# Norms by two float32r products and a full-width inverse root, and operands a multiple of 64 bytes apart

## The chip, the cores and the metric

The kernel runs on one core of a Trainium2 chip (trn2). TensorE (PE) multiplies, VectorE (DVE), ScalarE (ACT) and GpSimd (POOL) work on tiles of 128 partitions, and SyncE (SP) issues most DMAs. The metric is the device time of one execution in microseconds; lower is better.

## The reference

One decoder layer over a sequence of 1024 tokens with 1024 features, in float32. Six of its steps are RMS norms over the features of x:

```python
def rms_norm(x, g):
    xf = x.astype(jnp.float32)
    y = xf * lax.rsqrt(jnp.mean(xf * xf, axis=-1, keepdims=True) + NORM_EPS)
    return (y * g.astype(jnp.float32)).astype(x.dtype)

def swiglu(u, w_in, w_out):
    gate, up = jnp.split(u @ w_in, 2, axis=-1)
    return (jax.nn.silu(gate) * up) @ w_out

# reference(), one layer
f1 = swiglu(rms_norm(h, ffn1_pre_g[l]), ffn1_w_in[l], ffn1_w_out[l])
h = h + HALF_STEP * rms_norm(f1, ffn1_post_g[l])
u = rms_norm(h, mix_pre_g[l])
p_rwkv, p_swa, q_mem, gate_logits = _split(u @ w_in[l], IN_SIZES)
...
mem_n = rms_norm(mem, mem_norm_g[l])
...
h = h + rms_norm(merged @ w_out[l], mix_post_g[l])
f2 = swiglu(rms_norm(h, ffn2_pre_g[l]), ffn2_w_in[l], ffn2_w_out[l])
h = h + HALF_STEP * rms_norm(f2, ffn2_post_g[l])
```

The mixer between them has three branches: a recurrence over 64-feature heads (RWKV-7), windowed attention and attention into 256 memory tokens `mem`. NORM_EPS is 1e-6; the feed-forward width is 2816.

## The kernel before

Activations lie feature-major: a tile holds 128 features (partitions) of 512 tokens (columns), and x is eight such tiles for each half h of the sequence. A weight product is done in three float32r products (`mm3`, L327 to L332): the weight and the moving operand are each split into a rounded part (`hi`) and its remainder (`lo`), the copy to `hi` on ScalarE, the subtraction to `lo` on VectorE (`split` L392, `operand` L261), and hi·hi, hi·lo and lo·hi are summed in PSUM. Weights come through five staging buffers (`w_raw`) and up to eight split operands (`w_hi`, `w_lo`), each for twelve products.

The stages follow each other: the norm of `mem` with its keys and values, the first FFN (nine column blocks of its gate products first, `ffn_in_gate`, then the rest; its output in seven forms, `ffn_outs`, summed by `ffn_out_sum`), the mixer, the output projection (`pw`), the second FFN, whose last output form runs for two quarters of 256 columns (TAIL), so that the last norm covers only 256 columns.

A norm over x has these steps. `sum_squares` (L396) squares the eight tiles on ScalarE and adds them on VectorE. `rstd` (L358) then sums over the 128 partitions by products: for each 128 columns the squares are the stationary operand and a column of ones the moving one (`ps_ms`, L365), so that the sums come out as a column on 128 partitions, four columns for 512 tokens. Thirteen small VectorE instructions on 128 x 4 elements make the inverse root (a start from the bit pattern, three Newton steps); in the last stage (`quick`) a reciprocal, ScalarE's Sqrt and one step. Four products with the identity (`ps_rs`, L387) then spread the roots over all partitions, into PSUM. `pre_norm` (L410), `factors_norm` (L441) and `post_norm` (L719) multiply each tile by its gain and by this bank; `post_norm` adds the residual and stores. There are thirteen such norms: eleven over 512 columns, two over 256 in the tail; `mem` has one of its own (`start`).

The operands of `ps_ms` and `ps_rs` are float32. The tile framework orders the instructions of each engine by a priority: inside `high_priority` they are put ahead by `self.lead` or `self.urgent`, and `keep_in_program_order` keeps those it is given in the written order. `between` is work that PE is given between the two blocks of a norm, at the start and in the tail. PSUM has eight banks: four with the tag `mm` (`px`, `py`, `pr`, `pq`, `pw`, `po` and others), four for the rest.

Tiles of a pool lie one behind the other in SBUF, so a pool's addresses depend on the sizes before it. `ones` and `gn_eps` are tiles of one float32 column.

Of the kernel before, what the change touches and what calls it, by code (L numbers as in the profile page):

```python
# [10 lines left out]
F32 = mybir.dt.float32  # L11
F32R = mybir.dt.float32r
I32 = mybir.dt.int32
ALU = mybir.AluOpType
ACT = mybir.ActivationFunctionType
AXX = mybir.AxisListType.X

P = 128
T = 1024
TH = 512  # L20
D = 1024
# [3 lines left out]
MEM = 256  # L25
EPS = 1e-6
# [72 lines left out]
class WindowBlock(Block):  # L99
# [10 lines left out]
    def scores(self):  # L110
        nc, V, S, k = self.nc, self.nc.vector, self.nc.scalar, self.k
        self.w0 = P if self.b == 0 else 0
# [3 lines left out]
        for kv in (0, 1):  # L116
            for q in (0, 1):
                ps = k.psum("sc")
                rows = slice(q * 64, q * 64 + 64)
                for j in (0, 1):  # L120
                    last = self.mm(ps[:, j * n : (j + 1) * n], self.qs[rows, kv * 2 + j], self.kd[kv][rows, kcols])
                i = (kv * 2 + q) * 2
                V.scalar_tensor_tensor(sc[:, i : i + 2, :n], ps[:, : 2 * n].rearrange("p (j k) -> p j k", k=n), 0.125,
                                       k.wmask[:, self.w0:].rearrange("p k -> p () k").broadcast_to([P, 2, n]), ALU.mult, ALU.add)
        st = self.pool.tile([P, 5, 8], F32, tag="st", name="st", bufs=2)
        V.tensor_reduce(st[:, 0], sc[:, :, :n], AXX, ALU.max)
        V.tensor_tensor(st[:, 0], st[:, 0], k.sinks, ALU.max)
        V.tensor_scalar(st[:, 1], st[:, 0], -1.0, None, ALU.mult)
        V.tensor_tensor(st[:, 2], k.sinks, st[:, 0], ALU.subtract)
        S.activation(st[:, 2], st[:, 2], ACT.Exp)  # L130
# [77 lines left out]
class Builder:  # L208
# [146 lines left out]

    def rstd(self, sqs, width, pool, n=TH, columns=False, quick=False, between=None):  # L358
        nc = self.nc
        V = nc.vector  # L360
        nb = n // P
        ps = self.psum("ps_ms")
        for j in range(nb):
            for i, sq in enumerate(sqs):
                mm = nc.tensor.matmul(ps[:, j : j + 1], sq[:, j * P : (j + 1) * P], self.ones, start=i == 0, stop=i == len(sqs) - 1)  # L365
                if between:
                    self.tc.keep_in_program_order(mm)
        m, y, hm, q = (pool.tile([P, 4], F32, tag="rs" + t, name="rs" + t, bufs=2)[:, :nb] for t in "myhq")
        with self.tc.high_priority(offset=self.lead):
            V.tensor_scalar(m, ps[:, :nb], 1.0 / width, EPS, ALU.mult, ALU.add)  # L370
            if quick:
                V.reciprocal(y, m)
                nc.scalar.activation(y, y, ACT.Sqrt)
            else:
                V.tensor_scalar(y.bitcast(I32), m.bitcast(I32), 1, None, ALU.logical_shift_right)
                V.tensor_scalar(y.bitcast(I32), y.bitcast(I32), -1, 0x5F3759DF, ALU.mult, ALU.add)
            V.tensor_scalar(hm, m, -0.5, None, ALU.mult)
            for _ in range(1 if quick else 3):
                V.tensor_tensor(q, y, y, ALU.mult)
                V.tensor_tensor(q, q, hm, ALU.mult)  # L380
                V.scalar_tensor_tensor(y, q, 1.5, y, ALU.add, ALU.mult)
        if between:
            between()
        out = self.psum("ps_rs")
        with self.tc.high_priority(offset=self.lead):
            for j in range(nb):
                mm = nc.tensor.matmul(out[:, j * P : (j + 1) * P], y[:, j : j + 1].broadcast_to([P, P]), self.ident, start=True, stop=True)  # L387
                if between:
                    self.tc.keep_in_program_order(mm)
        return (out, y) if columns else out  # L390

    def split(self, x, hi, lo):  # L392
        self.nc.scalar.copy(hi, x)  # L393
# [2 lines left out]
    def sum_squares(self, xs, pool):  # L396

        nc = self.nc
        n = xs[0].shape[1]
        acc = None  # L400
        for x in xs:
            sq = pool.tile([P, n], F32, tag=f"sq{n}", name="sq", bufs=3)
            nc.scalar.activation(sq, x, ACT.Square)
            if acc is None:
                acc = sq
            else:
                nc.vector.tensor_tensor(acc, acc, sq, ALU.add)
        return acc

    def pre_norm(self, x, part, gname, u, pool):  # L410

        h, lo, hi = part
        xs = [t[h][:, lo:hi] for t in x]
        rs = self.rstd([self.sum_squares(xs, pool)], D, pool, hi - lo)[:, : hi - lo]
        for k in range(KD):
            if lo == 0:
                u[k][h] = self.u_tile(), self.u_tile()
            t = pool.tile([P, TH], F32, tag="un", name="un", bufs=2)[:, : hi - lo]
            self.nc.vector.scalar_tensor_tensor(t, xs[k], self.vec(gname, k), rs, ALU.mult, ALU.mult)
            self.split(t, *(y[:, lo:hi] for y in u[k][h]))  # L420
# [20 lines left out]
    def factors_norm(self, xs, part, gname, pool, between=None, then=None):  # L441

        h, lo, hi = part
        xs = [x[h][:, lo:hi] for x in xs]
        rs = self.rstd([self.sum_squares(xs, pool)], D, pool, hi - lo, between=between)[:, : hi - lo]
        for k in range(KD) if then else (0, 4, 1, 5, 2, 6, 3, 7):
            self.nc.vector.scalar_tensor_tensor(xs[k], xs[k], self.vec(gname, k), rs, ALU.mult, ALU.mult)
            if then:
                then(k)
# [269 lines left out]
    def post_norm(self, acc, part, gcol, xr, pool, save=None):  # L719

        nc = self.nc
        h, lo, hi = part
        cols = slice(h * TH + lo, h * TH + hi)
        xs = [acc[k][h][:, lo:hi] for k in range(KD)]
        end = save is self.io["out"]
        with self.tc.high_priority(offset=self.urgent if end else 0):
            sq = self.sum_squares(xs[KH:] + xs[:KH] if h else xs, pool)
        rs = self.rstd([sq], D, pool, hi - lo, quick=end, between=self.between if end else None)[:, : hi - lo]
        for k in range(KD):
            nc.vector.scalar_tensor_tensor(xs[k], xs[k], gcol(k), rs, ALU.mult, ALU.mult)  # L730

            e = nc.gpsimd if end and cols.stop == T and k in (0, 2, 4) else nc.vector
            e.tensor_tensor(xs[k], xs[k], xr[k], ALU.add)
            if save is not None:
                nc.sync.dma_start(save[:, k, cols], xs[k])
# [5 lines left out]
    def mixer_consts(self, cp):  # L741
        nc, io = self.nc, self.io
        V = nc.vector
# [15 lines left out]
        for q in (0, 64):  # L759
            for i, op in ((0, ALU.is_gt), (1, ALU.is_ge)):  # L760
                m = self.gmask[q : q + 64, i, :]
# [23 lines left out]
        m = self.wmask[:, :P]  # L785
        nc.gpsimd.affine_select(m, m, [[1, P]], ALU.is_gt, NEG, base=0, channel_multiplier=-1)
        m = self.wmask[:, P:]
        nc.gpsimd.affine_select(m, m, [[-1, P]], ALU.is_ge, NEG, base=0, channel_multiplier=1)
        self.gn_eps = cp.tile([P, 1], F32, name="gn_eps")
        V.memset(self.gn_eps, GN_EPS)  # L790


# [394 lines left out]
    def start(self, x, pool, km_d, vm_d):  # L1187
        nc, tc, io = self.nc, self.tc, self.io
        V = nc.vector
        keep = tc.keep_in_program_order  # L1190
        send = self.send = lambda *a: keep(nc.sync.dma_start(*a))
        mm = lambda *a, start, stop: keep(nc.tensor.matmul(*a, start=start, stop=stop))
# [7 lines left out]
        def load_x(h, a):  # L1200
            for k in range(a, a + KH):
                send(x[k][h], io["xT"][:, k, h * TH : (h + 1) * TH])
# [32 lines left out]
        def mem_squares():  # L1235
            out = []
            for a in (0, KH):
                sq = pool.tile([P, KH, MEM], F32, tag="mem_sq", name="mem_sq", bufs=1)
                s = pool.tile([P, MEM], F32, tag="mem_ss", name="mem_ss", bufs=2)
                nc.scalar.activation(sq, mem[:, a : a + KH], ACT.Square)  # L1240
                V.tensor_tensor(sq[:, :2], sq[:, :2], sq[:, 2:], ALU.add)
                V.tensor_tensor(s, sq[:, 0], sq[:, 1], ALU.add)
                out.append(s)
            return out
# [12 lines left out]
        sqs = mem_squares()  # L1257
# [5 lines left out]
        keys(2)  # L1263
        load_strip()
        load_x(1, 0)
        ps, col = self.rstd(sqs, D, pool, MEM, True, between=while_mem)
        load_x(1, KH)
        rs = pool.tile([P, MEM], F32, name="mem_rs", bufs=1)
        nc.scalar.copy(rs, ps[:, :MEM])
        for h in range(4):  # L1270
            t = pool.tile([P, MEM], F32, tag="km", name="km", bufs=2)
# [5 lines left out]
        for i in (0, 1):  # L1277
            t = pool.tile([P, 512], F32, tag="mkv", name="vm", bufs=3)
# [249 lines left out]
    def build(self):  # L1528
        nc, tc, io = self.nc, self.tc, self.io
        with contextlib.ExitStack() as outer, tc.tile_pool(reuse_waits="tile", name="consts", bufs=1) as cp, \  # L1530
# [5 lines left out]
            nc.scalar.dma_start(self.vecs, io["vecs"])  # L1536
            self.ones = cp.tile([P, 1], F32, name="ones")
            nc.vector.memset(self.ones, 1.0)
            self.ident = cp.tile([P, P], F32, name="ident")
            nc.gpsimd.memset(self.ident, 1.0)  # L1540
            nc.gpsimd.affine_select(self.ident, self.ident, [[1, P]], ALU.is_equal, 0.0, base=0, channel_multiplier=-1)
# [16 lines left out]
            with quarters() as self.qpool:  # L1558
                x = self.acc_tiles()
# [17 lines left out]
            with quarters() as self.qpool:  # L1577
                merged = self.last_branches(*mixed)
                x = self.acc_tiles()
# [90 lines left out]
```

## Time and profile before

| | |
|---|---|
| median of three runs | 2317.04 us (2313.6 to 2322.88) |
| the profiled execution | 2322.86 us, its span 2321.1 us |
| granted TensorE clock | 0.997 |
| busy share of the span | PE 98%, DVE 71%, ACT 41%, POOL 4% |
| HBM | 179 GB/s over the span |

Durations below come from the one profiled execution; the span runs from its first to its last instruction. A product's busy time has a modelled end, so distances between starts are used where PE's time is counted. A matmul of float32 operands appears as two passes in the trace, one of float32r as one.

### The profile page before, as it was taken

Reading aid. Unit: us, or ns where it says so; the run is one execution under the profiler, and the core shown is the slowest. Engines: PE = TensorE matmul, PEld = TensorE weight load, DVE = VectorE, ACT = ScalarE, POOL = GpSimd, SP = SyncE. Lnnn points to the kernel's source line nnn. Section 1 sums busy time; section 2 is a strip of 40 time slices with the busy share of each in tenths; the row PEclk is TensorE's granted clock in tenths of the full one; section 3 lists DMA queues with packets and bytes.
Section 4 is the critical chain, followed back from the end, with each engine's and each line's share of the span. In section 5 each row is a group of like instructions: output and inputs, shape, how many; then the busy total and the mean of one; then the engine's idle time right before and its main releaser. Section 6 shows DMA issues by size and latency. Waiting matters only on the chain. (4 is left out here: it accounts for less than half of the span.)

```text
span 2321.1 us, 33883 instructions
## 1 busy us (share of the span) xinstructions
PE 2278.9 (98%) x12080; PEld 1862.7 (80%) x12080; DVE 1653.6 (71%) x2790; ACT 962.3 (41%) x1791; POOL 95.7 (4%) x134
## 2 busy tenths in 40 slices
PE   8999999999999999999999999999999999999998
PEld 6778888888888777888878888778888778888887
DVE  6998666666688786895645466565899886666666
ACT  5522333454445544223444455234552223345451
POOL 0000000000000000001310000241000000000000
PEclk9999999999999999999999999999999999999999
DMA  8577545586644446325435425555467775558663
GB/s 276 160 251 255 171 158 166 171 289 207 190 160 144 111 118 186 131 96 183 139 130 179 129 95 170 173 178 160 158 212 229 263 243 172 168 182 271 214 195 114
DMA packets 280778, 417.70 MB, mean 180 GB/s; under 512 B 82304, under 2 KB 104320, under 8 KB 280352
## 3 DMA queue, kind: packets, MB, share of 16 engines
q1 hardware_dynamic: 231552, 388.20, 51.9%
q10 hardware_dynamic: 49056, 27.34, 4.2%
q8 instruction: 95, 1.56, 0.3%
q14 instruction: 75, 0.61, 0.1%
HBM read 284.89 MB, written 129.50 MB: 179 GB/s over the span
## 5 line engine op out<-in xcount | busy, mean ns | idle before, releaser
L264 ACT CAST w_hi<-w_raw 128x512 fp32r<-128x512 f32 x594 | 366.2, 620 | 774.8 <-PE px L331 140.9
L266 DVE TENSOR_TENSOR w_lo<-w_raw,w_hi 128x512 fp32r<-128x512 f32 x594 | 415.4, 702 | 218.0 <-ACT w_hi L264 181.1
L330 PE MATMUL po<-u,w_hi 128*128 128x512 f32 (+1 forms) x476 | 181.8, 382 | 0.0
L332 PE MATMUL po<-u,w_lo 128*128 128x512 f32 (+1 forms) x476 | 181.1, 380 | 0.0
L331 PE MATMUL po<-u,w_hi 128*128 128x512 f32 (+1 forms) x476 | 181.0, 380 | 0.0
L330 PE MATMUL pgate<-u,w_hi 128*128 128x512 f32 x384 | 155.2, 404 | 0.0
L332 PE MATMUL pgate<-u,w_lo 128*128 128x512 f32 x384 | 151.5, 394 | 0.0
L331 PE MATMUL pgate<-u,w_hi 128*128 128x512 f32 x384 | 149.7, 390 | 0.0
L330 PE MATMUL px<-f,w_hi 128*128 128x512 f32 x352 | 139.0, 395 | 6.4 <-DVE up L600 3.9
L330 PE MATMUL px<-u,w_hi 128*128 128x512 f32 x352 | 137.5, 391 | 3.0 <-ACT w_hi L264 2.1
L331 PE MATMUL pz<-u,w_hi 128*128 128x512 f32 x352 | 137.3, 390 | 0.6 <-DVE u L394 0.6
L331 PE MATMUL px<-f,w_hi 128*128 128x512 f32 x352 | 137.6, 391 | 0.0
L330 PE MATMUL pz<-u,w_hi 128*128 128x512 f32 x352 | 137.3, 390 | 0.3 <-DVE m L587 0.3
L332 PE MATMUL px<-f,w_lo 128*128 128x512 f32 x352 | 137.5, 391 | 0.0
L331 PE MATMUL px<-u,w_hi 128*128 128x512 f32 x352 | 137.0, 389 | 0.0
L332 PE MATMUL pz<-u,w_lo 128*128 128x512 f32 x352 | 137.0, 389 | 0.0
L332 PE MATMUL px<-u,w_lo 128*128 128x512 f32 x352 | 137.0, 389 | 0.0
L394 DVE TENSOR_TENSOR u<-hid,u 128x512 fp32r<-128x512 f32 x114 | 78.5, 689 | 49.2 <-ACT u L393 46.6
L331 PEld LDWEIGHTS po<-u,w_hi 128*128 128x128 f32 x476 | 89.5, 188 | 17.3
L332 PEld LDWEIGHTS po<-u,w_lo 128*128 128x128 f32 x476 | 89.5, 188 | 17.3
L330 PEld LDWEIGHTS po<-u,w_hi 128*128 128x128 f32 x476 | 89.5, 188 | 17.2
L393 ACT CAST u<-hid 128x512 fp32r<-128x512 f32 x114 | 70.7, 620 | 69.6 <-DMA hid<-form_d 61.8
(347 smaller groups left out, 5127.6 us busy)
## 6 DMA issues: line engine op xcount, KB each, us to landing
w_raw<-in_ffn_in SPq DMA_DIRECT2D x220, 256.0 KB
hid<-form_d SPq DMA_DIRECT2D x154, 256.0 KB
w_raw<-in_win SPq DMA_DIRECT2D x112, 256.0 KB
ws<-in_ffn_out SPq DMA_DIRECT2D x88, 256.0 KB
form_d<-g SPq DMA_DIRECT2D x88, 256.0 KB
ffn_sum_d<-ws SPq DMA_DIRECT2D x88, 256.0 KB
w_raw<-ffn_sum_d SPq DMA_DIRECT2D x88, 256.0 KB
form_d<-h SPq DMA_DIRECT2D x66, 256.0 KB
```

The source lines that it names most:

```text
L264: self.nc.scalar.copy(hi, x)
L266: self.nc.vector.tensor_tensor(lo, x, hi.bitcast(F32), ALU.subtract)
L330: mm(out, wh, xh, start=first, stop=False, **kw)
L331: mm(out, wh, xl, start=False, stop=False, **kw)
L332: mm(out, wl, xh, start=False, stop=last, **kw)
L393: self.nc.scalar.copy(hi, x)
L394: self.nc.vector.tensor_tensor(lo, x, hi.bitcast(F32), ALU.subtract)
```

## The change

The norms over x no longer use `rstd`, which remains for `mem` alone. A new `inverse_root` takes the sum of squares (128 x n), and

- splits it, with the epsilon added, into `sq_hi` (ScalarE) and `sq_lo` (VectorE);
- multiplies both by a constant 128 x 128 float32r matrix `mean_r` of 1/D, so that each row of the PSUM bank `ps_rs` holds the mean over all features: two float32r products of n columns;
- takes the logarithm of that bank and the exponential of -0.5 times it on ScalarE, n columns wide, with one table set loaded ahead (`preload_act_table_set`);
- refines by one Newton step (a square on ScalarE, two VectorE instructions), into the SBUF tile `rs`, from which the users read.

The products stand within `high_priority`; the hi and lo products stand in the written order only where there is a `between`. The squares' ring has four buffers instead of three and now holds `sq_hi`, `sq_lo` and `rs` as well. `gn_eps` and the new `eps` take 16 columns (64 bytes) each, of which one is used.

```diff
-    def rstd(self, sqs, width, pool, n=TH, columns=False, quick=False, between=None):
+    def rstd(self, sqs, width, pool, n, between):
...
+    def inverse_root(self, sq, pool, between=None):
+
+        nc = self.nc
+        n = sq.shape[1]
+        hi, lo, y = (pool.tile([P, n], t, tag=f"sq{n}", name=name, bufs=4) for t, name in ((F32R, "sq_hi"), (F32R, "sq_lo"), (F32, "rs")))
+        ps = self.psum("ps_rs")[:, :n]
+        V, S = nc.vector, nc.scalar
+        keep = self.tc.keep_in_program_order
+        with self.tc.high_priority(offset=self.lead):
+            keep(S.activation(hi, sq, ACT.Identity, bias=self.eps))
+            V.scalar_tensor_tensor(lo, sq, self.eps, hi.bitcast(F32), ALU.add, ALU.subtract)
+            keep(S.preload_act_table_set("natural_log_exp_and_others"))
+            for i, x in enumerate((hi, lo)):
+                mm = nc.tensor.matmul(ps, self.mean_r, x, start=i == 0, stop=i == 1)
                 if between:
-                    self.tc.keep_in_program_order(mm)
-        return (out, y) if columns else out
+                    keep(mm)
+            keep(S.activation(y, ps, ACT.Ln))
+            keep(S.activation(y, y, ACT.Exp, scale=-0.5))
+            keep(S.activation(sq, y, ACT.Square))
+            V.scalar_tensor_tensor(sq, ps, -0.5, sq, ALU.mult, ALU.mult)
+            V.scalar_tensor_tensor(y, sq, 1.5, y, ALU.add, ALU.mult)
+        if between:
+            between()
+        return y
...
-            sq = pool.tile([P, n], F32, tag=f"sq{n}", name="sq", bufs=3)
+            sq = pool.tile([P, n], F32, tag=f"sq{n}", name="sq", bufs=4)
...
-        rs = self.rstd([self.sum_squares(xs, pool)], D, pool, hi - lo)[:, : hi - lo]
+        rs = self.inverse_root(self.sum_squares(xs, pool), pool)
...
-        rs = self.rstd([self.sum_squares(xs, pool)], D, pool, hi - lo, between=between)[:, : hi - lo]
+        rs = self.inverse_root(self.sum_squares(xs, pool), pool, between)
...
-        rs = self.rstd([sq], D, pool, hi - lo, quick=end, between=self.between if end else None)[:, : hi - lo]
+        rs = self.inverse_root(sq, pool, self.between if end else None)
...
-        self.gn_eps = cp.tile([P, 1], F32, name="gn_eps")
+        self.gn_eps = cp.tile([P, 16], F32, name="gn_eps")[:, :1]
...
-        ps, col = self.rstd(sqs, D, pool, MEM, True, between=while_mem)
+        ps, col = self.rstd(sqs, D, pool, MEM, while_mem)
...
+            self.mean_r = cp.tile([P, P], F32R, name="mean_r")
+            nc.vector.memset(self.mean_r.bitcast(F32), 1.0 / D)
+            self.eps = cp.tile([P, 16], F32, name="eps")[:, :1]
+            nc.vector.memset(self.eps, EPS * D / P)
```

More of the change, by code (lines that the diff above doesn't have):

```diff
@@ L364, in rstd @@
             for i, sq in enumerate(sqs):
-                mm = nc.tensor.matmul(ps[:, j : j + 1], sq[:, j * P : (j + 1) * P], self.ones, start=i == 0, stop=i == len(sqs) - 1)
-                if between:
-                    self.tc.keep_in_program_order(mm)
+                keep(nc.tensor.matmul(ps[:, j : j + 1], sq[:, j * P : (j + 1) * P], self.ones, start=i == 0, stop=i == len(sqs) - 1))
         m, y, hm, q = (pool.tile([P, 4], F32, tag="rs" + t, name="rs" + t, bufs=2)[:, :nb] for t in "myhq")
@@ L370, in rstd @@
             V.tensor_scalar(m, ps[:, :nb], 1.0 / width, EPS, ALU.mult, ALU.add)
[L371 to L376, printed above, removed]
+            V.tensor_scalar(y.bitcast(I32), m.bitcast(I32), 1, None, ALU.logical_shift_right)
+            V.tensor_scalar(y.bitcast(I32), y.bitcast(I32), -1, 0x5F3759DF, ALU.mult, ALU.add)
             V.tensor_scalar(hm, m, -0.5, None, ALU.mult)
-            for _ in range(1 if quick else 3):
+            for _ in range(3):
                 V.tensor_tensor(q, y, y, ALU.mult)
@@ L381, in rstd @@
                 V.scalar_tensor_tensor(y, q, 1.5, y, ALU.add, ALU.mult)
-        if between:
-            between()
+        between()
         out = self.psum("ps_rs")
@@ L386, in rstd @@
             for j in range(nb):
-                mm = nc.tensor.matmul(out[:, j * P : (j + 1) * P], y[:, j : j + 1].broadcast_to([P, P]), self.ident, start=True, stop=True)
-                if between:
-                    self.tc.keep_in_program_order(mm)
-        return (out, y) if columns else out
+                keep(nc.tensor.matmul(out[:, j * P : (j + 1) * P], y[:, j : j + 1].broadcast_to([P, P]), self.ident, start=True, stop=True))
+        return out, y
+    def inverse_root(self, sq, pool, between=None):
[4 more added lines that the diff above has]
+        V, S = nc.vector, nc.scalar
+        keep = self.tc.keep_in_program_order
+        with self.tc.high_priority(offset=self.lead):
[4 more added lines that the diff above has]
+                mm = nc.tensor.matmul(ps, self.mean_r, x, start=i == 0, stop=i == 1)
+                if between:
+                    keep(mm)
[5 more added lines that the diff above has]
+        if between:
+            between()
+        return y
     def split(self, x, hi, lo):
```

## The prediction

> **What bounds the kernel now.** I read the page first, then TensorE's waits, then the timeline around single norms.
>
> ```profile
> span 2321.1 us, 33883 instructions
> PE 2278.9 (98%) x12080; PEld 1862.7 (80%) x12080; DVE 1653.6 (71%) x2790; ACT 962.3 (41%) x1791; POOL 95.7 (4%) x134
> PEclk9999999999999999999999999999999999999999
> ...
> PE ps_ms L365 <- DVE sq L407: 3.1, 3, 1.6
> ...
> PE ps_rs L387 <- DVE rsy L381: 2.2, 4, 1.4
> ```
>
> TensorE (PE) is busy for 98% of the span at full granted clock, and stands only some microseconds for the norm: 3.1 for the sum of squares, 2.2 for the root. So the kernel is a queue of products: time goes where a product leaves that queue, or where PE is made to stand. VectorE (DVE, 71%) and ScalarE (ACT, 41%) matter only where they make PE stand, and in the tail after the last product.
>
> The page's busy time has modelled ends, so I count PE time from start to start. Two places in the timeline, one for each kind of norm product:
>
> ```profile
> 1667.40 0.39 PE L331 MATMUL px<-u,w_hi 128*128 128x512 f32 x1
> 1667.63 0.39 PE L332 MATMUL px<-u,w_lo 128*128 128x512 f32 x1
> 1668.13 1.02 PE L365 MATMUL ps_ms<-ones,sq 128*128 128x1 f32 x8
> 1669.01 0.48 PE L330 MATMUL px<-u,w_hi 128*128 128x512 f32 x1
> 1669.33 0.39 PE L331 MATMUL px<-u,w_hi 128*128 128x512 f32 x1
> ...
> 2259.75 0.39 PE L331 MATMUL po<-u,w_hi 128*128 128x512 f32 x1
> 2259.97 0.39 PE L332 MATMUL po<-u,w_lo 128*128 128x512 f32 x1
> 2260.20 1.05 PE L387 MATMUL ps_rs<-ident,rsy 128*128 128x128 f32 x8
> 2261.01 0.48 PE L330 MATMUL po<-u,w_hi 128*128 128x512 f32 x1
> 2261.33 0.39 PE L331 MATMUL po<-u,w_hi 128*128 128x512 f32 x1
> ```
>
> A float32r product of 512 columns starts 0.23 us after the one before it. Around 2260.20 the step from 2259.97 to 2261.33 is 1.36 us and holds two such products (0.46) and one block of norm products: the block costs 0.90 us. In it are eight passes (four float32 products, two passes each), and the first float32r product behind them takes 0.32 instead of 0.23. Around 1668.13 the same sum gives 1.70 - 0.46 = 1.24: 0.90 and a wait of 0.34.
>
> **The change, part by part.**
>
> *Products removed.* `rstd` issues two blocks for each norm over x: `ps_ms` (the mean) and `ps_rs` (the spread of the root over 128 rows). There are thirteen such norms: eleven of 512 columns, two of 256 in the tail. That is 22 blocks at 0.90 = 19.8 us, and four blocks of half the passes. Of these the tail's last two stand behind the last weight product and are counted below; the other two are taken at half, 0.45 each. Together 20.7 us off PE's queue. Mem's norm keeps its blocks.
>
> *Products added.* Each norm gets two float32r products of the same width as its columns, 0.23 us each at 512: 11 x 0.46 = 5.1; the 256 wide pair in the middle of the tail about 0.23. Together 5.3 us. They have the form of the products around them, so the 0.09 us behind a float32 block is gone, and is in the 0.90. Net off PE: 15.4 us.
>
> *Waits at the norm's products.* Before, PE stands for the sum of squares ahead of `ps_ms` and for `rsy` ahead of `ps_rs`; after, for `sq_hi` (ScalarE) and `sq_lo` (VectorE). In the built order most `sq_hi` products are moved forward to where their sum of squares is just ready, and `sq_lo` follows two or three products (0.5 to 0.7 us) behind, about one VectorE instruction of that width. Two meeting points stay two; I set the change at nothing, with 6 us to the good (all of 24 waits of about 0.25) and 6 to the bad.
>
> *The chain to the root.* Rows for its parts, the last two from VectorE's timeline:
>
> ```profile
> L403 ACT ACTIVATE sq<-acc 128x512 f32<-128x512 f32 x88 | 54.3, 630 | 27.4 <-DVE acc L733 9.7 <-DVE acc L685 8.0 <-DVE sq L407 7.8
> ...
> L403 ACT ACTIVATE sq<-acc 128x256 f32<-128x256 f32 x16 | 6.6, 417 | 30.8 <-DVE acc L685 28.6 <-DVE sq L407 1.2 <-DVE rsm L370 0.9
> ...
> L882 ACT ACT_TABLE_LOAD x4 | 5.1, 1283 | 0.1
> ...
> L407 DVE TENSOR_TENSOR sq<-sq 128x512 f32<-128x512 f32 x77 | 53.0, 689 | 9.8 <-ACT sq L403 6.6
> ...
> L730 DVE SCALAR_TENSOR_TENSOR acc<-acc,post,ps_rs 128x512 f32<-128x512 f32 x24 | 17.0, 741 | 1.5 <-PE ps_rs L387 1.5
> ...
> L381 DVE SCALAR_TENSOR_TENSOR rsy<-rsq,rsy 128x4 f32<-128x4 f32 x31 | 5.0, 162 | 1.0
> ...
> 2311.81 0.16 DVE L380 TENSOR_TENSOR rsq<-rsq,rsh 128x2 f32<-128x2 f32 x1
> 2312.01 0.16 DVE L381 SCALAR_TENSOR_TENSOR rsy<-rsq,rsy 128x2 f32<-128x2 f32 x1
> ```
>
> Before: 0.9 of PE, thirteen small VectorE instructions that wait for each other (0.16 each, 0.20 apart: 2.5), 0.9 of PE: 4.3 us. After: `sq_hi` 0.63, `sq_lo` 0.69, product 0.4, logarithm, exponential and square 0.63 each, two instructions of VectorE 0.74 + 0.69: 5.0 us. So the result is some 0.7 us later when nothing else is queued. For VectorE itself 2.5 us of small work become 2.1 of wide work, and eight users read the root from SBUF instead of PSUM (0.74 against 0.69), 0.4 us less: no loss. ScalarE gains 4 x 0.63 and sixteen more table loads (16 become 32 in the built program) of 1.28: 11 x 2.5 + 2 x 1.7 + 20.5 = 51 us in 2321, and it is 41% busy. Its copies `w_hi` run up to eight operands ahead, and an operand lasts twelve products, 2.7 us; a chain of 5 us is covered. Behind the logarithm, which waits for PE's product, stand such copies, and in the gate stage the copies of `px` that free PE's banks. No DMA is added or moved to another queue; ScalarE's own stores of mem's keys and values start later by the chain, and are read in the attention, long after. The chain is not covered where ScalarE is full, nor where PE soon reads what the norm made. The first rows are three stretches with the busy time of each engine, the last two from the timeline:
>
> ```profile
> core 0: us, PE busy (x) PEld busy (x) DVE busy (x) ACT busy (x) POOL busy (x), PEclk, DMA share, GB/s
> 41.00:62.00 21.00, 19.25 (x88) 15.81 (x89) 14.56 (x28) 14.26 (x25) 0.00 (x0) 1.00 0.63 214
> ...
> 690.00:745.00 55.00, 54.39 (x253) 44.52 (x253) 46.74 (x94) 26.72 (x48) 1.12 (x2) 1.00 0.45 144
> 1600.00:1662.00 62.00, 61.43 (x286) 50.56 (x285) 45.93 (x91) 30.50 (x54) 0.00 (x0) 1.00 0.48 153
> ...
> 737.38 0.39 PE L330 MATMUL pr<-u,w_hi 128*128 128x512 f32 x1
> ...
> 738.62 1.29 DVE L394 TENSOR_TENSOR u<-un,u 128x512 fp32r<-128x512 f32 x2
> ```
>
> From 41 to 62 us ScalarE has 14.3 of 21 us. From 690 to 745 VectorE has 46.7 of 55, and the last two tiles of `u` are split at 739.9, while `pr`, begun at 737.38, reads the last of them after 21 products, at 742.2: 2.3 us of slack. Between the norm before it and this place PE loses two to four of its own blocks, 1.3 us each net, which were part of the cover; where that is more than the slack and the chain isn't shorter, PE stands. I take 1.5 us in all; bounds 0 and 6 (the four norms there at 1.5).
>
> *The tail.* Behind the last weight product there is no cover:
>
> ```profile
> 2309.80 0.43 DVE L407 TENSOR_TENSOR sq<-sq 128x256 f32<-128x256 f32 x1 [0.54 <-ACT sq L403]
> 2310.38 0.58 PE L365 MATMUL ps_ms<-ones,sq 128*128 128x1 f32 x4 [1.58 <-DVE sq L407]
> ...
> 2313.04 1.26 DVE L730 SCALAR_TENSOR_TENSOR acc<-acc,post,ps_rs 128x256 f32<-128x256 f32 x3 [0.87 <-PE ps_rs L387]
> ```
>
> From the end of the sum (2310.23) to its first user is 2.81 us. After: `sq_hi` 0.42, then the table load 1.28 (longer than `sq_lo` and the products beside it), three ScalarE steps of 0.42, two of VectorE at about 0.43, and handoffs of about 0.1 in all: 3.9 to 4.1. Plus 1.2 us.
>
> Does a load cost more than its row? Two rows of a switch:
>
> ```profile
> 52.25 1.28 ACT L566 ACT_TABLE_LOAD   x1
> 53.55 0.63 ACT L566 ACTIVATE g<-g 128x512 f32<-128x512 f32 x1
> ```
>
> The next instruction starts 1.30 us after the load does. The Trainium skill, "ScalarE: Activation LUTs", What ACT_TABLE_LOAD costs, adds a drain of some 1.38 us to each switch, 2.66 together. By that the tail would lose 2.6 us instead of 1.2; the trace shows no such drain here, and I go by it.
>
> *Addresses.* In the built program nearly all weights and moving operands start 32 bytes past a multiple of 64, before and after. Of the float32r weight products only 191, all of `form` tiles, read a moving operand at a multiple of 64 itself, so at an odd multiple of 32 bytes from their weights; after, none does.
>
> ```profile
> L331 PE MATMUL po<-u,w_hi 128*128 128x512 f32 x436 | 169.7, 389 | 0.0
> ...
> L331 PE MATMUL po<-form,w_hi 128*128 128x512 f32 x136 | 53.5, 393 | 0.2 <-DVE form L394 0.2
> ```
>
> 4 ns on 3 x 136 products is 1.6 us to gain. By the Trainium skill, "SBUF — State Buffer", Door 1 (lines of 16 bytes), 32 bytes more or less would change nothing; then this term is zero.
>
> *Sum.* -15.4 + 0 + 1.5 + 1.2 - 1.6 = -14.3 us. The profiled execution took 2322.86 (span 2321.1), the slowest of the three runs; 2308.6 / 2322.86 = 0.9938, and on the median of 2317.04 that is 2302.8.
>
> **Rivals.**
>
> *Slower: the norm's chain becomes the bound.* Eight norms stand one behind the other, each fed by what the last one made: four at the end of the first FFN, four from the mixer's end into the second. In the new chain five of the steps cross between ScalarE, VectorE and PE, and both engines take their work in order. If each step waits for one or two copies ahead of it (0.63 each), that is about 4 us a norm, 1 more with the 0.7 and less cover: PE stands 5 us at each, 40 in all. The sum without standing is -15.8, so this gives +24, 2341 on the median. Even is 2.0 us a norm, slower by 0.5% is 3.4. For it: VectorE at 74% and 85% in those two stretches. Against it: before, PE's waits for the norm are 5.3 us in the whole kernel, with thirteen dependent steps. 7%. By the rule of the Trainium skill on the drain, named above, each of the sixteen loads would hold ScalarE 1.38 longer, and this case would be likelier.
>
> *No change: PE's time is freed and stood away.* VectorE sets the pace in those eight norms and takes as long as before, so that the 1.3 us off PE at each is lost again (10 us): -15.8 + 10 = -5.8, 2311. For it: the 2.3 us of slack above. Against it: in the built order the first of the eight has its `sq_hi` 47 products (10.7 us) earlier than `ps_ms` stood, so its chain begins sooner. 24%.
>
> *More than forecast: the waits go too.* All 6 us of them vanish: -20.3, 2296.8. It lies within the forecast's own range.
>
> **How the numbers follow.** Forecast 69% (its own range 2296 to 2308), no change 24%, slower 7%. A difference under 0.5% (11.6 us) is about what a measurement of this kernel can't tell from none. The forecast lies at -0.6%, and a tenth of its chance above 2305.4, inside that bound: faster 0.62, same 0.31, slower 0.07. The range takes in the good bound and the no-change case: 2294 to 2315.
>
> **What would show it.** In the profile after: no `ps_ms` but mem's; 26 products on `mean_r`, steps of 0.23 around them; from the last sum to the first user in the tail about 4 us; 32 table loads of 1.28; ScalarE near 1010 us; `po<-form` at 389 ns. Wrong it would be if PE's waits for `u`, `sq_hi`, `sq_lo` or `w_hi` grew beyond 10 us in all, or if the steps of the weight products changed from 0.23.

## The result: slower, and the profile after

The changed kernel takes 2357.89 us (median; 2353.72 to 2358.58), against 2316.8 us for the kernel before in the same series: a ratio of 1.017, 95% interval 1.0146 to 1.0194. The forecast was 2302.8 with a range of 2294 to 2315.

The page of the kernel after:

```profile
span 2356.1 us, 33492 instructions
PE 2309.7 (98%) x11914; PEld 1848.6 (78%) x11914; DVE 1658.9 (70%) x2683; ACT 1007.8 (43%) x1856; POOL 94.4 (4%) x134
PEclk9999999999999999999999999999999999999999
```

Lines of PE's waits in it (us in total, times, longest):

```profile
PE px L330 <- DVE u L604: 9.5, 4, 8.0
...
PE pr L330 <- ACT raw L820: 5.3, 2, 3.1
PE ps_rs L397 <- ACT sq_hi L393: 2.7, 2, 2.0
```

There are 166 PE instructions fewer, as the change says, but PE is busy 31 us longer, at much the same granted clock (0.994 against 0.997). So the time went into the products themselves. The group of `po` on `u`, which took 389 ns before:

```profile
L331 PE MATMUL po<-u,w_hi 128*128 128x512 f32 x436 | 172.1, 395 | 0.0
```

PE's timeline of the kernel after at three places:

```profile
1755.61 0.39 PE L331 MATMUL pz<-u,w_hi 128*128 128x512 f32 x1
...
1757.94 0.40 PE L332 MATMUL pz<-u,w_lo 128*128 128x512 f32 x1
1766.34 0.80 PE L330 MATMUL px<-f,w_hi 128*128 128x512 f32 x1 [8.01 <-DVE u L604]
1766.94 0.63 PE L331 MATMUL px<-f,w_hi 128*128 128x512 f32 x1
1767.36 0.63 PE L332 MATMUL px<-f,w_lo 128*128 128x512 f32 x1
...
2286.15 0.40 PE L332 MATMUL po<-u,w_lo 128*128 128x512 f32 x1
2286.39 0.40 PE L397 MATMUL ps_rs<-sq_hi,mean_r 128*128 128x512 f32 x1
2286.62 0.39 PE L397 MATMUL ps_rs<-sq_lo,mean_r 128*128 128x512 f32 x1
2286.85 0.39 PE L330 MATMUL po<-u,w_hi 128*128 128x512 f32 x1
```

From 1755.61 to 1757.94 ten products start in 2.33 us: 233 ns a step (from the start of one product to the start of the next), where the kernel before has 227 (table further on). Around 2286.39 the norm's two products follow at the step of their neighbours: the norm itself costs PE what was forecast. At 1766.34 PE stands for 8 us, a wait that the kernel before does not have, and restarts with steps of 0.42 us.

The following table takes the same weight products in each kernel, by number, and gives the time from the first to the last of each stretch. The stretches are named by their times in the kernel before. Two kernels that are told below stand beside the two.

| stretch of the kernel before | before | after | e1 | e7 |
|---|---|---|---|---|
| 0 to 55 | 48.4 | 46.8 | 47.1 | 46.4 |
| 55 to 112 | 57.0 | 56.2 | 57.0 | 54.0 |
| 112 to 240 | 127.9 | 128.6 | 130.7 | 127.9 |
| 240 to 625 (no norm) | 385.0 | 394.4 | 384.8 | 384.9 |
| 625 to 735 (four norms) | 110.1 | 105.8 | 104.7 | 104.1 |
| 735 to 1190 | 455.0 | 467.5 | 458.2 | 456.1 |
| 1190 to 1540 | 349.9 | 352.6 | 347.6 | 348.6 |
| 1540 to 1705 (four norms) | 165.0 | 159.9 | 157.4 | 158.1 |
| 1705 to 1765 | 60.0 | 72.9 | 71.2 | 66.5 |
| 1765 to 2240 | 475.2 | 482.8 | 474.0 | 474.8 |
| 2240 to the last product | 68.3 | 66.4 | 67.1 | 66.4 |
| last product to the end | 12.6 | 15.1 | 15.1 | 15.1 |

Two things stand out. From 240 to 625 us there is no norm at all, and 1693 products take 9.4 us more. And 1705 to 1765 us takes 12.9 us more, over twice the 5.1 that the four norms ahead of it saved.

### The profile page after: what moved, and what is told of

Its sections match the earlier page's. It is cut to its first block, busy times and chain, and to the rows that moved or that the text cites. A ratio compares the mean times of both kernels' runs of the same rounds, so it can differ in the third digit from the quotient of the medians.

```text
span 2356.1 us, 33492 instructions
## 1 busy us (share of the span) xinstructions
PE 2309.7 (98%) x11914; PEld 1848.6 (78%) x11914; DVE 1658.9 (70%) x2683; ACT 1007.8 (43%) x1856; POOL 94.4 (4%) x134
## 5 line engine op out<-in xcount | busy, mean ns | idle before, releaser
L332 PE MATMUL po<-u,w_lo 128*128 128x512 f32 (+1 forms) x476 | 183.4, 385 | 0.0
L331 PE MATMUL po<-u,w_hi 128*128 128x512 f32 (+1 forms) x476 | 183.2, 385 | 0.0
L330 PE MATMUL pgate<-u,w_hi 128*128 128x512 f32 x384 | 157.4, 410 | 0.0
L332 PE MATMUL pgate<-u,w_lo 128*128 128x512 f32 x384 | 153.3, 399 | 0.0
L331 PE MATMUL pgate<-u,w_hi 128*128 128x512 f32 x384 | 151.8, 395 | 0.0
L331 PE MATMUL px<-f,w_hi 128*128 128x512 f32 x352 | 140.2, 399 | 0.3 <-DVE f L411 0.2
L332 PE MATMUL px<-f,w_lo 128*128 128x512 f32 x352 | 139.9, 398 | 0.0
L331 PE MATMUL pz<-u,w_hi 128*128 128x512 f32 x352 | 139.5, 396 | 0.0
L331 PE MATMUL px<-u,w_hi 128*128 128x512 f32 x352 | 139.1, 396 | 0.4 <-DVE u L411 0.4
L332 PE MATMUL pz<-u,w_lo 128*128 128x512 f32 x352 | 139.2, 395 | 0.0
L332 PE MATMUL px<-u,w_lo 128*128 128x512 f32 x352 | 139.1, 395 | 0.0
L411 DVE TENSOR_TENSOR u<-hid,u 128x512 fp32r<-128x512 f32 x114 | 78.4, 689 | 46.4 <-ACT u L410 45.4
L332 PEld LDWEIGHTS po<-u,w_lo 128*128 128x128 f32 x476 | 89.4, 188 | 19.8
L331 PEld LDWEIGHTS po<-u,w_hi 128*128 128x128 f32 x476 | 89.4, 188 | 19.8
```

The source lines that it names most:

```text
L330: mm(out, wh, xh, start=first, stop=False, **kw)
L331: mm(out, wh, xl, start=False, stop=False, **kw)
L332: mm(out, wl, xh, start=False, stop=last, **kw)
L411: self.nc.vector.tensor_tensor(lo, x, hi.bitcast(F32), ALU.subtract)
```

## Experiments on the step of a product

In the built programs the change moves the weight strips, which lie on the left side of SBUF behind the constants, by 576 bytes (`mean_r` 512, `eps` 64). The tiles of `u`, `acc`, `f` and `r2` lie on the right side and stay. So the distance from a product's weights to its moving operand goes, for 8076 of the weight products of 512 columns, from 0 to 192 modulo 256 bytes (the 8084 of the next expectation count eight of the norm's own products as well). Theory A: that distance sets the step. The rivals were the weights' own address (B), the new work of ScalarE and VectorE or the clock (C), and the longer chain of the norms (D).

**e1_eps_wider**

```diff
-            self.eps = cp.tile([P, 16], F32, name="eps")[:, :1]
+            self.eps = cp.tile([P, 64], F32, name="eps")[:, :1]
```

> The kernel after with its eps tile 64 elements wide instead of 16, so that everything allocated behind it on the left, the weight strips among it, moves up by 192 bytes and the moving tiles on the right stay. Theory A (the step of a weight product is set by the distance in bytes of its moving operand from its weights, modulo 256: 227 ns at 0, about 233 ns at 192): 8084 products return from distance 192 to 0, the step of 512 columns from 233.3 to 227 ns, the time falls by about 46 us to 2300 to 2315 us, below before. Theory C (the new norm's instructions on ScalarE and VectorE, or the lower granted clock, slow TensorE): nothing changes, 2358 us, steps of 233 ns. Theory D (the chain of norms grew): 2358 us.

Measured: 2322.37 us, 1.001 of before (0.9999 to 1.0022). Some 35 us come back (37 by the two ratios to before) with only a tile's width changed. Its group of `po` on `u`, and a line of PE's waits:

```profile
L331 PE MATMUL po<-u,w_hi 128*128 128x512 f32 x436 | 169.8, 389 | 0.0
```

```profile
PE px L330 <- DVE u L604: 10.5, 3, 8.3
```

The step is back, and C and D fall as causes of the slower step. But 2300 to 2315 was expected: the kernel only draws level with the one before. The wait on VectorE is still there; the second group of experiments is about that.

**e2_before_64**, the other way round: the kernel before, with nothing but its addresses changed.

```diff
-            self.ones = cp.tile([P, 1], F32, name="ones")
+            self.ones = cp.tile([P, 24], F32, name="ones")[:, :1]
```

> The kernel before with its tile of ones 24 elements wide instead of 1 (a 64-byte shift of all that lies behind it on the left); no instruction changes. Theory A: 8082 products go from distance 0 to 192 modulo 256, steps of 227 to 233 ns, so about 46 us more: 2355 to 2365 us. Theory C and D: no change, 2317 us.

Measured: 2360.51 us, 1.0172 (1.0157 to 1.0187). A loss as large as that of the change appears in the kernel before by 64 bytes of padding (its group by line):

```profile
L331 PE MATMUL po<-u,w_hi 128*128 128x512 f32 x436 | 172.2, 395 | 0.0
```

**e3_after_right_pad**

```diff
+            outer.enter_context(tc.tile_pool(name="pad", bufs=1, side="right")).tile([P, 48], F32, name="pad")
             self.upool = outer.enter_context(tc.tile_pool(reuse_waits="tile", name="u", bufs=32, side="right"))
```

> The kernel after with an unused tile of 192 bytes laid first on the right side, so that the moving tiles on the right move down by 192 bytes and the weights stay where the change put them (32 modulo 256). Theory A (the distance): back at distance 0, steps of 227 ns, the same time as the kernel with the wider eps tile, 2300 to 2315 us. Theory B (the weights' own address modulo 256 sets the step): 233 ns, 2358 us. Theory C: 2358 us.

Measured: 2324.32 us, 1.0014 (1.0004 to 1.0024), the same group at 389 ns. The time misses 2300 to 2315 as e1 did, by the same wait (8.3 us). The weights lie where the change put them and the step is 227: B falls, the distance counts.

**e4_before_128**

```diff
-            self.ones = cp.tile([P, 1], F32, name="ones")
+            self.ones = cp.tile([P, 40], F32, name="ones")[:, :1]
```

> The kernel before with its tile of ones 40 elements wide: the weights move up by 128 bytes, and 8108 products go from distance 0 to 128 modulo 256. Theory A with a period of 256: some other step, by its form bad or worse than at 64 (229.1) and 192 (233.3): 231 to 236 ns, 2345 to 2380 us. If the period is 128 the step stays 227 ns and the time 2317 us. Theory C: 2317 us.

Measured: 2355.93 us, 1.0149 (1.0132 to 1.0166). A distance of 128 is bad as well: the period is not 128.

**e10_distance_64 and e11_distance_224**, the same edit with 56 and 16 elements, one run each, so without an interval.

> The kernel before with its tile of ones 56 elements wide: the weights move up by 192 bytes, and 8076 products go from distance 0 to 64 modulo 256. By the 191 products at 64 in the kernels run so far (229.1 and 230.5 ns): 229 to 231 ns and 2333 to 2350 us. A rule that any multiple of 64 bytes is as good as another gives 227 ns and 2320 us.

> The kernel before with its tile of ones 16 elements wide: the weights move up by 32 bytes, and 8080 products go to distance 224 modulo 256, an odd multiple of 32. By the 187 products at 32 (233.7 ns): 231 to 236 ns, 2350 to 2395 us. If only multiples of 64 matter, it is at least as slow as the kernels at 64, 128 and 192.

Measured: 2337.68 and 2364.11 us, beside 2321.87 for the kernel before in the same series. Both lie in the ranges expected. The mean step, from the start of a product of 512 columns to the start of the next, over all that follow one another within 245 ns:

| distance modulo 256 | step, ns | products | kernel |
|---|---|---|---|
| 0 | 227.1 | 8252 | before (e1 and e3 as well) |
| 64 | 229.5 | 7850 | e10 |
| 128 | 232.7 | 7865 | e4 |
| 192 | 233.3 | 7882 | after (e2 as well) |
| 224 | 233.3 | 7867 | e11 |

"A multiple of 64" is no rule here: 128 and 192 are about as bad as an odd multiple of 32. In the kernel before 8076 of the 8252 lie at 256 modulo 512 and the other 176 at 0, with 227.1 and 227.2 ns: 256 is the period as far as these runs go. 96 and 160 were not run as whole kernels.

**e9_low_part_64 and e5_all_distances** ask whose weights count.

```diff
-        lo = pool.tile([P, 4, P], F32R, tag="w_lo", name="w_lo", bufs=bufs)
+        lo = pool.tile([P, 4 * P + 64], F32R, tag="w_lo", name="w_lo", bufs=bufs)
+        lo = lo[:, 16 : 16 + 4 * P].rearrange("p (k c) -> p k c", k=4)
```

> The kernel before with only the low part of each weight strip laid 64 bytes further on; the moving tiles and the high parts stay. Of the three products of a block the first (high weights, next high) keeps distance 0 to its own and the next weights, the second (high weights, next low) has 0 and 192, the third (low weights, next high) 192 and 0, modulo 256. Theory A1 (own weights): steps 227, 227, 233, about 2332 us. Theory A2 (the weights loaded meanwhile): 227, 233, 227, about 2332 us. Theory A3 (neither alone; products hold each other up over several steps, as the mixed kernel's 230 ns at distance 0 suggests): all three between 227 and 233.

Measured: 2347.26 us in one run. The groups by line (lines are one further on, since a line was added: L331 and L332 use high weights, L333 low ones):

```profile
L333 PE MATMUL po<-u,w_lo 128*128 128x512 f32 x436 | 173.0, 397 | 0.0
L332 PE MATMUL po<-u,w_hi 128*128 128x512 f32 x436 | 170.9, 392 | 0.0
L331 PE MATMUL po<-u,w_hi 128*128 128x512 f32 x436 | 170.0, 390 | 0.0
```

The mean steps are 228.6 ns after the first product (0 to its own and the next weights), 229.3 after the second (0 and 192) and 235.4 after the third (192 and 0). So it is mostly the product's own weights, as A1 has it, and A2 falls. But no theory fits as it stood: A1 and A2 both gave 2332 us, 15 less than measured, the neighbours are not untouched, and 235.4 is more than the 233.3 of a kernel that has 192 throughout (A3 had all three between 227 and 233).

```diff
-        return self.upool.tile([P, TH], dtype, tag="u", name="u")
+        return self.upool.tile([P, TH + 8], dtype, tag="u", name="u")[:, :TH]
```

> The kernel before with each of the 32 buffers of u made 32 bytes longer, so that the moving tiles of u lie at all eight multiples of 32 bytes modulo 256, and with the low part of each weight strip (w_lo) laid 64 bytes further on than the high part. It is read only from the trace, as a table of the step of a product by the distance of its moving operand from its own weights and from those of the product behind it, which are loaded meanwhile. Theory A1 (a product is slowed by its own weights' distance): rows with the same distance to their own weights agree whatever the next weights are. Theory A2 (the weights loaded meanwhile, those of the next product): rows with the same distance to the next weights agree. By the four distances seen so far: 227 ns at 0, 229 to 231 at 64, 233 at 32, 128 and 192.

With this edit on top of e9's, 2353.17 us in one run. The distances are mixed from product to product, and the clear steps are gone: 852 products at 0 to both weights take 230.2 ns on average, the worst pair (32 and 96) 234.4, all together 231.7. A single product's distance does not give its step when its neighbours have others. What in the chip does this stays open; that the distance in a whole kernel is worth 34 to 40 us is shown by e1, e2 and e3.

## Experiments on the wait at 1741 us

With the addresses mended (e1), PE's last weight product starts only 1.9 us earlier than in the kernel before, and the tail is 2.5 us longer. Up to 1705 us PE had gained 10.6 us, 7.6 of it in the four norms from 1540 on; then it stands. PE's timeline of e1:

```profile
1732.36 0.39 PE L332 MATMUL pz<-u,w_lo 128*128 128x512 f32 x1
1741.10 0.80 PE L330 MATMUL px<-f,w_hi 128*128 128x512 f32 x1 [8.35 <-DVE u L604]
```

`px` must be read by VectorE's line 604 before the next product may overwrite it. That operation in VectorE's timeline, in e1 and in the kernel before:

```profile
1740.34 0.70 DVE L604 TENSOR_TENSOR u<-px,m 128x512 f32<-128x512 f32 x1
```

```profile
1740.72 0.68 DVE L587 TENSOR_TENSOR u<-px,m 128x512 f32<-128x512 f32 x1
```

It stands behind the factors of the last norm. PE came earlier, VectorE did not. VectorE's timeline there, first the kernel before, then e1 (in brackets: idle before, and what ended it):

```profile
1695.68 0.69 DVE L407 TENSOR_TENSOR sq<-sq 128x512 f32<-128x512 f32 x1
1697.58 0.16 DVE L370 TENSOR_SCALAR rsm<-ps_ms 128x4 f32<-128x4 f32 x1 [1.21 <-PE ps_ms L365]
...
1702.27 2.72 DVE L447 SCALAR_TENSOR_TENSOR acc<-acc,vecs,ps_rs 128x512 f32<-128x512 f32 x4 [0.25 <-PE ps_rs L387]
```

```profile
1695.85 1.49 DVE L424 TENSOR_TENSOR sq<-sq 128x512 f32<-128x512 f32 x2
...
1700.89 0.69 DVE L266 TENSOR_TENSOR w_lo<-w_raw,w_hi 128x512 fp32r<-128x512 f32 x1
1704.37 0.69 DVE L403 SCALAR_TENSOR_TENSOR sq<-ps_rs,sq 128x512 f32<-128x512 f32 x1 [2.78 <-ACT sq L402]
...
1706.78 4.72 DVE L464 SCALAR_TENSOR_TENSOR acc<-acc,vecs,rs 128x512 f32<-128x512 f32 x7
```

From the end of the sum of squares to the first user it is 5.9 us before (1696.37 to 1702.27) and 9.4 in e1 (1697.34 to 1706.78). VectorE stands 2.78 us at line 403 for ScalarE's Square, and its queue, full up to 1741, stands behind that. At the norm before this one (1665 us) it is 5.4 against 10.2 us, with 2.79 us of the same wait. Why Square is late is seen in ScalarE's timeline of e1:

```profile
1697.59 0.72 ACT L393 ACTIVATE sq_hi<-sq,eps 128x512 fp32r<-128x512 f32 x1
1698.33 1.28 ACT L395 ACT_TABLE_LOAD   x1
1699.75 0.60 ACT L400 ACTIVATE rs<-ps_rs 128x512 f32<-128x512 f32 x1
1700.24 0.61 ACT L264 CAST w_hi<-w_raw 128x512 fp32r<-128x512 f32 x1
1700.75 0.64 ACT L401 ACTIVATE rs<-rs 128x512 f32<-128x512 f32 x1
1701.40 1.28 ACT L583 ACT_TABLE_LOAD   x1
1702.70 0.63 ACT L583 ACTIVATE g<-g 128x512 f32<-128x512 f32 x1
1703.24 0.57 ACT L578 COPY m<-px 128x512 f32<-128x512 f32 x1
1703.70 0.63 ACT L402 ACTIVATE sq<-rs 128x512 f32<-128x512 f32 x1
```

Between the exponential (line 401) and Square (line 402) a gate's Silu is put, with its table load and a copy: 2.3 us. Theory E: this chain, through VectorE's full queue, is what PE waits for at 1741. Four kernels with e1's wider tile:

**e7_square_on_vector**

```diff
-            keep(S.activation(sq, y, ACT.Square))
+            V.tensor_tensor(sq, y, y, ALU.mult)
```

> The kernel with the wider eps tile, with the Square of the correction computed on VectorE (one more operation of 0.69 us there) instead of ScalarE, so that nothing of the norm stands behind the table load that follows the exponential. The same arithmetic otherwise. Theory E: the two idle stretches of VectorE of 2.8 us in front of the correction go, three or four operations of 0.69 us come, the wait at 1741 falls from 8.5 to 4 to 7 us and the time to 2317 to 2321 us. Rival E2 (only VectorE's amount of work counts, not its waits): wait 10 to 11 us, 2324 us. Rival F: unchanged, 2322 us.

Measured: 2312.27 us, 0.9965 of before (0.9951 to 0.9979). VectorE's timeline at the same norm:

```profile
1682.13 3.07 DVE L424 TENSOR_TENSOR sq<-sq 128x512 f32<-128x512 f32 x4
...
1689.16 0.69 DVE L402 TENSOR_TENSOR sq<-rs 128x512 f32<-128x512 f32 x1
1689.88 0.69 DVE L403 SCALAR_TENSOR_TENSOR sq<-ps_rs,sq 128x512 f32<-128x512 f32 x1
1690.60 0.69 DVE L404 SCALAR_TENSOR_TENSOR rs<-sq,rs 128x512 f32<-128x512 f32 x1
1691.33 1.41 DVE L464 SCALAR_TENSOR_TENSOR acc<-acc,vecs,rs 128x512 f32<-128x512 f32 x2
```

And the line of PE's waits:

```profile
PE px L330 <- DVE u L604: 6.6, 4, 3.8
```

The chain is 6.1 us (1685.20 to 1691.33), VectorE has more to do and is done earlier, and the longest wait falls from 8.3 to 3.8. E2, by which only the amount counts, falls. The time fell by more than expected: 4.7 us from 1705 to 1765, and 3.0 from 55 to 112 us, where another norm stands among gates.

**e6_no_correction**

```diff
-            keep(S.activation(sq, y, ACT.Square))
-            V.scalar_tensor_tensor(sq, ps, -0.5, sq, ALU.mult, ALU.mult)
-            V.scalar_tensor_tensor(y, sq, 1.5, y, ALU.add, ALU.mult)
```

> The kernel with the wider eps tile (weights and moving tiles a multiple of 256 bytes apart), with the correction step behind the exponential left out of each norm (ScalarE's Square and VectorE's two operations; the root is then the plain exponential). Theory E (from the norm at 1638 us to the factors at 1741 us VectorE's stream is the bound; there the new norm takes 7 to 10 us from its last sum to its first use against 4 to 6 before, because Square stands behind another table load and VectorE behind Square, and TensorE's lead of 10.6 us ends in a wait of 8.5 us): the wait at 1741 falls to 0 to 4 us and the time from 2322 to 2311 to 2318 us. Rival F (TensorE waits there for a weight strip or another transfer): wait and time unchanged, 2322 us.

Measured: 2308.37 us, 0.994 (0.9927 to 0.9952), 2.6 us below the range expected. PE's waits:

```profile
PE ps_rs L397 <- ACT sq_hi L393: 6.8, 5, 2.3
...
PE px L330 <- DVE u L601: 3.1, 3, 1.5
```

At the place of the 8.35 us wait 0.6 is left, and PE's last weight product starts 15.4 us earlier than in the kernel before. F, a wait for some transfer, falls.

**e8_old_norms_late**: the four norms between 1609 and 1705 us by the old `rstd` (put back as `rstd_old`; its text and the wider tile are left out here).

```diff
-        rs = self.inverse_root(self.sum_squares(xs, pool), pool, between)
+        if gname == "ffn2_pre_g":
+            rs = self.rstd_old([self.sum_squares(xs, pool)], D, pool, hi - lo, between=between)[:, : hi - lo]
+        else:
+            rs = self.inverse_root(self.sum_squares(xs, pool), pool, between)
...
+        if save is self.h2:
+            rs = self.rstd_old([sq], D, pool, hi - lo)[:, : hi - lo]
+        else:
+            rs = self.inverse_root(sq, pool, self.between if end else None)
```

> The kernel with the wider eps tile, with the norms of the mixer's output and of the second feed-forward's input (four, between 1609 and 1705 us) computed as in the kernel before, the others as in the kernel after. Theory E (what TensorE gains by these four norms is lost at the wait at 1741 us): TensorE reaches that point some 9 us later, the wait of 8.5 us is gone, and the time stays 2322 us (2318 to 2324). Rival G (the gain of the new norm counts at each place): 8 to 10 us slower, 2330 us.

Measured: 2319.2 us, 0.9989 (0.998 to 0.9998); the stretch 1540 to 1705 takes 164.1 us, 6.7 more than in e1, 1705 to 1765 takes 60.2, 11.0 less, and the wait is gone. So the change gained nothing by these four norms: E stands, G falls.

**e12_old_last_norm**: e7, with the very last norm as before. Its lines 784 and 787 are lines 747 and 750 of e7.

```diff
-        rs = self.inverse_root(sq, pool, self.between if end else None)
+        if end and cols.stop == T:
+            rs = self.rstd_old([sq], D, pool, hi - lo, quick=True, between=self.between)[:, : hi - lo]
+        else:
+            rs = self.inverse_root(sq, pool, self.between if end else None)
```

> The kernel with the wider eps tile and Square on VectorE, with the last norm (the second half of the last part, behind which only the output is left) computed as in the kernel before. The end from the last weight product to the end of the span took 12.6 us before and 15.2 us with the new norm: if that is the new norm's chain (two table loads, hi and lo, two exponentials in turn), the end falls by 2 to 3 us and the time from 2312 to 2309 to 2311 us. If the end is set by the transfers of the output, it stays 2312 us.

Measured: 2309.91 us, 0.9951 of before (0.9937 to 0.9965): the fastest kernel with all of the computation, though its interval overlaps that of e7. The tail is 13.0 us instead of 15.1. From the end of the sum to the first user it is 3.2 us instead of 4.1, and from there to the end of the last of the eight users 5.0 instead of 6.5: the larger part of the gain is theirs, and not the chain's, which the expectation named. First users of the root in VectorE's timeline of e7 (line 747) and of e12, and GpSimd beside them in e12:

```profile
2300.66 1.75 DVE L747 SCALAR_TENSOR_TENSOR acc<-acc,post,rs 128x256 f32<-128x256 f32 x3
...
2302.66 1.36 DVE L747 SCALAR_TENSOR_TENSOR acc<-acc,post,rs 128x256 f32<-128x256 f32 x2
```

```profile
2300.75 1.27 DVE L784 SCALAR_TENSOR_TENSOR acc<-acc,post,ps_rs 128x256 f32<-128x256 f32 x3 [1.32 <-PE ps_rs L413]
...
2302.29 0.86 DVE L784 SCALAR_TENSOR_TENSOR acc<-acc,post,ps_rs 128x256 f32<-128x256 f32 x2
```

```profile
2301.36 1.59 POOL L787 TENSOR_TENSOR acc<-acc,x_re 128x256 f32<-128x256 f32 x2 [730.88 <-DMA x_re<-h]
```

## Why the prediction was wrong

*Addresses, the step that failed.* It was sized at -1.6 us, as if only the 191 `form` products could change, on the reading that weights and moving operands "start 32 bytes past a multiple of 64, before and after". That is a residue modulo 64; what counts is the distance modulo 256. The `form` products were slow before because they lay at 32, and the rest fast because they lay at 0, which the change undid. Its measure is e1 against after: 35 us the other way. The one row that the step rested on (393 against 389 ns, a group of which only a part lies at 32) did show that an address has a price, and it was carried over to 191 products where it held for all. The prediction's own sign of this error, steps other than 0.23, was too coarse: 227 and 233 ns both round to 0.23. The zero drawn there from the Trainium skill ("SBUF — State Buffer", Door 1) was the prediction's own step: the section speaks of lines of 16 bytes and not of the distance between two operands, and e2 differs from before by 64 bytes and takes 40 us more. A sentence of the Trainium skill, "TensorE: Matmul & The Clock Gate", Step-by-step: what each phase is for, says that loading the next weights takes nothing from the running product, since each has its own read port. It does not cover this either: which weights lie where against the moving operand changes the step here by 6 ns of 227, and in e9 it is mostly the product's own weights, not the next ones.

*The chain to the root, mis-sized.* Forecast: 0.7 us later when nothing else is queued, 1.5 us of standing in all, at most 6. Measured in e1: 3.5 us later at 1698 and 4.8 at 1665, one wait of 8.35 us, and up to the last weight product PE idle for 10.8 us more than in the kernel before (41.9 against 31.1). The prediction saw that copies may stand behind the logarithm, but not that a Silu with its table load may come between exponential and Square, nor that VectorE's queue then stands at line 403. It looked for cover near the mixer's start and took the gate stage as covered. The rival "no change", by which VectorE sets the pace and PE's gain is stood away, held for the four late norms (7.6 us gained in e1, 11.2 lost in the next 60 us) but less for the four at 625 to 735: they gained 5.4, and the stretch behind them, to 1190, takes 3.2 more, for a reason that these runs do not show.

*What was right.* PE's gain: -15.4 net was forecast, and PE's last weight product is 15.4 earlier in e6, 13.7 in e7. That e6 agrees to the tenth is luck: e6 leaves out the correction, and PE is idle in it for 1.7 us more than in the kernel before (32.9 against 31.1), so its queue itself is some 17 us shorter. The waits at the norm's products, set at nothing, were 5.3 us before and are 4.7 in e1. The tail's chain: 3.9 to 4.1 was forecast from sum to first user, and it is 4.08 (VectorE's and ScalarE's timeline of the kernel after):

```profile
2342.26 0.42 DVE L424 TENSOR_TENSOR sq<-sq 128x256 f32<-128x256 f32 x1 [0.54 <-ACT sq L420]
...
2346.76 1.74 DVE L747 SCALAR_TENSOR_TENSOR acc<-acc,post,rs 128x256 f32<-128x256 f32 x3
```

```profile
2343.24 1.28 ACT L395 ACT_TABLE_LOAD   x1
2344.53 0.38 ACT L400 ACTIVATE rs<-ps_rs 128x256 f32<-128x256 f32 x1
```

The tail still grew by 2.5 instead of 1.2 us, because the eight users, from the first one's start to the last one's end, take 6.5 us instead of 5.0 (the first three 1.74 instead of 1.26; why, below). The 32 loads of 1.28 us and ScalarE's 1007.8 us are as forecast; behind the load at 2343.24 the next instruction starts 1.29 us later, again without the drain that the Trainium skill ("ScalarE: Activation LUTs", What ACT_TABLE_LOAD costs) adds. `po<-form` stayed at 393 ns instead of 389: its 191 products went from a distance of 32 to one of 64, and not to 0.

## What to carry over

Before a constant, a pad or a pool is added to a kernel that is bound by products, compare the distance from weights to moving operands modulo 256 bytes in both built programs; here 0 is worth 1.5 to 1.8% of the whole time over 128, 192 or 224, and a wider pad on either side gives it back. When an activation is moved onto ScalarE, follow what the scheduler puts between its steps: here a table switch between two steps of a chain, with a full queue on VectorE behind it, cost 10 us in all (e1 against e7). PE's saved time counts only as far as the next place where it meets the engine that paid for it.

## What the runs showed of the hardware

- The step of a float32r product of 512 columns depends on the distance from weights to moving operand: 227.1 ns at 0, 229.5 at 64, 232.7 to 233.3 at 128, 192 and 224 modulo 256, in kernels where nearly all products have the same distance. Where neighbours differ (e9, e5), the same distance gives other steps.
- Behind a wait of 8 us PE restarts slowly: in after, steps of 0.42 us at 1766.94 instead of 0.23. In e1 the granted clock is 0.75 in the ten us from 1741, and 1.00 in the ten after them. So the stretch from 1705 to 1765 us of the table takes 11.2 us more for a wait of 8.35.
- VectorE's product with the root in SBUF takes 1.75 us for three beside GpSimd's sums, with the root in PSUM 1.27. The Trainium skill, "SBUF — State Buffer", Who interferes with whom, says that a VectorE instruction with two SBUF inputs contends with a GpSimd instruction that reads SBUF; the rows agree. In both kernels the last of the eight, with no GpSimd sum beside it, takes 0.47, so the place of the root alone is not what costs.
